# Second MLP product of an encoder layer: seven block products in place of eight, weight blocks summed by accumulating transfers

## The chip, the core and the metric

The kernel runs on one core of one Trainium2 chip. The metric is the device time of one execution in microseconds (us), taken as the median of several runs. The core has a matmul engine (PE, with its weight loads shown apart as PEld), a vector engine (DVE), an engine for activations and copies (ACT), a general engine (POOL) and a queue processor (SP) that here only starts transfers. Each engine works through its own instructions strictly in the order in which they were written; between engines they wait for each other by semaphores.

## The reference, cut to what matters

The program is one layer of an encoder on 512 tokens of width 1024. The change concerns its last stage, a squared-ReLU MLP of 4096 hidden features:

```python
h = rmsnorm(x, g_pre_mlp[l]) * (1.0 + sc2) + sh2                  # 512 x 1024
f = jnp.square(jax.nn.relu(h @ w_mlp1[l])) @ w_mlp2[l]            # 1024 -> 4096 -> 1024
x = x + gt2 * rmsnorm(f, g_post_mlp[l])
```

All of it is float32. A product in full precision is made of three matmuls: each operand is split into a high part of fewer bits and the low rest, and high by high, high by low and low by high are summed.

## The kernel before, in words

The kernel is recorded as a list of operations with their buffers. A planner (`Plan.order`) then walks through a model of the five engines: at each step it takes, of the operations whose inputs are ready and whose buffer slots are free, the one that can start first, and among those that can start at about the same time the one with the longest path behind it. What comes out is a fixed order for each engine. Its costs are lines of a small function (`_cost`); for a transfer it counts the issue, 0.65 us, the bytes at 360 GB/s, and 1.05 us until it has landed. An operation recorded on `vp` is one for DVE that the planner may give to POOL where it ends sooner there. All matmuls that write one PSUM bank share one priority.

A weight tile of 128 x 512 is loaded by SP (`wload`), split into `whi` by a copy on ACT and into `wlo` by a subtraction on DVE (`lo_of`), and used by PE. `mm3` writes the three matmuls of one product. Buffers have tags with a number of slots each (`NB`): split weights take slots of `w` (9) and `wx` (12), temporaries of `cv` (22).

The MLP works in two halves of 2048 features. In each half, four chunks of 512 features are computed (banks `pm`; 96 matmuls of 512 columns a chunk, in the first chunk 192 of 256): ReLU on ACT into `r`, square on `vp`, and the split into `gh` on ACT and `gl` on `vp`. Then `w_2` is multiplied in two column halves (banks `pf`): for each of 16 tiles of 128 features the split hidden values of four token tiles are the stationary operands and the split weight tile is the moving one, so a pair `whi`, `wlo` feeds 4 x 3 matmuls. In all that is 2 x 2 x 16 x 4 x 3 = 768 matmuls of 512 columns. The first half is copied from PSUM to `fA` by ACT, the second is added to it by DVE. At the end, for each token tile, the sum of squares is taken by ACT, the gain `G2` is multiplied in by DVE, a root and a reciprocal follow, and two DVE instructions scale the two column halves and add the residual `xr`; SP stores each half.

Of the kernel before, what the change touches and what calls it, by code (L numbers as in the profile page):

```python
# [220 lines left out]


class Op:
    __slots__ = ("eng", "call", "dur", "lat", "preds", "succs", "bufs", "new", "n", "rt", "start", "prio", "idx", "move", "urgent", "table", "port", "alt")


class Plan:
# [4 lines left out]
    def __init__(self, nc):  # L232
        self.nc, self.ops, self.tags, self.cnt = nc, [], {}, 0
        self.bias = self.local = 0.0
        self.pools = {}


# [15 lines left out]
    def record(self, eng, call, writes, reads, dur, lat=0.0, after=()):  # L253
        op = Op()
        op.eng, op.call, op.idx = eng, call, len(self.ops)
        op.dur, op.lat, op.move, op.urgent, op.table = dur, lat, None, self.local, None
        op.port, op.alt = eng == "gp", None
        preds = set(after)
        for v in reads:
            for q, box in v.b.writes:  # L260
                if _meet(box, v.box):
                    preds.add(q)
        for v in writes:
            for lst in (v.b.writes, v.b.reads):
                for q, box in lst:
                    if _meet(box, v.box):
                        preds.add(q)
        for v in writes:

            v.b.writes = [(q, box) for q, box in v.b.writes if not _within(box, v.box)]  # L270
            v.b.reads = [(q, box) for q, box in v.b.reads if not _within(box, v.box)]
            v.b.writes.append((op, v.box))
        for v in reads:
            v.b.reads.append((op, v.box))
        preds.discard(op)
        op.preds, op.succs = list(preds), []
        op.bufs = list({id(v.b): v.b for v in list(writes) + list(reads)}.values())
        op.new = []
        for b in op.bufs:
            if b.left == 0:  # L280
                op.new.append(b)
                self.tags[b.pool, b.tag]["order"].append(b)
            b.left += 1
            self.pools[b.pool]["left"] += 1
        op.prio = self.bias
        self.ops.append(op)
        return op


    def order(self):  # L290
# [14 lines left out]
        top = {}  # L305
        for op in ops:
            if op.eng == "pe":
                b = id(op.bufs[0])
# [246 lines left out]
def tile_hymba_layer(ctx, tc, t, out):  # L555
    nc = tc.nc
    plan = Plan(nc)

    FILTERS, INPUT, SOON, ROUND = 200.0, 1000.0, 9000.0, 3000.0
# [803 lines left out]


    w_1, w_2 = t["w_mlp1"][0], t["w_mlp2"][0]
    htag = (["cv"] * 3 + ["vx"]) * 6 + ["cv", "cv", "vx", "vx", "vx", "vx", "H", "vx"]
    hn = [0]

    def hidden_tile(s):
        hn[0] += 1  # L1370
        return R(htag[hn[0] % 32], s)

    fA, sq = {}, {}
    G2 = [S("G", "G2"), S("G", "G2")]
    late2 = ada_bcast(5120, t["g_post_mlp"][0], G2, ("ra",))
    step(late2)
    for half in range(2):
        hid = []
        for cc in range(4):
            c0 = half * 2048 + cc * 512  # L1380
            banks = PS4(cc + 1, "pm")
            ws = [wload(w_1[k * P:(k + 1) * P, c0:c0 + 512]) for k in range(8)]
            for th in range(2) if half == 0 and cc == 0 else (None,):
                ts = slice(0, 512) if th is None else slice(th * 256, th * 256 + 256)
                for k in range(8):
                    for i in range(4):
                        s = slice(i * P, (i + 1) * P)
                        mm3(banks[i][:, ts], ws[k][0][:, s], ws[k][1][:, s], h2T[k][0][:, ts], h2T[k][1][:, ts], k == 0, k == 7)
            for i in range(4):
                r = S("cv", "r")  # L1390
                act.activation(r, banks[i], AF.Relu)
                vp.tensor_tensor(out=r, in0=r, in1=r, op=ALU.mult)
                hi, lo = hidden_tile("gh"), hidden_tile("gl")
                act.copy(hi, r)
                lo_of(vp, lo, r, hi)
                hid.append((hi, lo))
            step(late2)
        for hf in range(2):
            cs = slice(hf * 512, hf * 512 + 512)
            banks = PS4(hf + 1, "pf")  # L1400
            nk = 8 if (half, hf) == (1, 1) else 16
            for k in range(nk):
                r0 = half * 2048 + k * P
                wh, wl = wload(w_2[r0:r0 + P, cs])
                for tt in range(4):
                    s = slice(tt * P, (tt + 1) * P)
                    mm3(banks[tt], hid[k][0][:, s], hid[k][1][:, s], wh, wl, k == 0, k == 15)
            if nk < 16:
                ws = [wload(w_2[half * 2048 + k * P:half * 2048 + (k + 1) * P, cs]) for k in range(nk, 16)]
            for tt in range(4):  # L1410
                s = slice(tt * P, (tt + 1) * P)
                for k in range(nk, 16):
                    mm3(banks[tt], hid[k][0][:, s], hid[k][1][:, s], ws[k - nk][0], ws[k - nk][1], False, k == 15)
                a = fA.get((tt, hf))
                if half == 0:
                    a = fA[tt, hf] = S("H", "fA")
                    act.copy(a, banks[tt])
                    continue
                dve.tensor_tensor(out=a, in0=banks[tt], in1=a, op=ALU.add)
                if hf == 0:  # L1420

                    q = sq[tt] = T1("sf")
                    act.activation(junk, a, AF.Square, accum_out=q[:, 0:1])
                    dve.tensor_scalar(out=q[:, 1:2], in0=q[:, 0:1], scalar1=1.0 / D, scalar2=EPS, op0=ALU.mult, op1=ALU.add)
                    vp.tensor_tensor(out=a, in0=a, in1=G2[0], op=ALU.mult)
                    continue
                q, g = sq[tt], S("cv", "g")
                act.activation(junk, a, AF.Square, accum_out=q[:, 2:3])
                dve.tensor_tensor(out=g, in0=a, in1=G2[1], op=ALU.mult)
                act.activation(q[:, 3:4], q[:, 2:3], AF.Sqrt, bias=q[:, 1:2], scale=1.0 / D)  # L1430
                dve.reciprocal(q[:, 4:5], q[:, 3:4])
                for i, a in enumerate((fA[tt, 0], g)):
                    dve.scalar_tensor_tensor(out=a, in0=a, scalar=q[:, 4:5], in1=xr[tt, i], op0=ALU.mult, op1=ALU.add)
                    sp.dma_start(out2d[tt * P:(tt + 1) * P, i * 512:(i + 1) * 512], a)

    done = plan.order()
    with tc.manual_schedule():
# [39 lines left out]
```

## Time and profile before

| | us |
|---|---|
| median of 3 runs (751.42 to 752.01) | 751.7 |
| the profiled execution | 750.51 |
| its span, first to last instruction | 748.7 |

The profile lists busy time by engine, groups of instructions by operation and tile, the chain of waits that ended last, and windows of the span. A name such as `pf<-whi,gh` reads: written tile, then what was read. All operations are issued from one helper line (L513), so tiles, not lines, tell the groups apart. The MLP begins at 375 us (first `pm` matmul) and is almost alone on PE from 396 us to the end.

### The profile page before, as it was taken

Reading aid. Unit: us, or ns where it says so; the run is one execution under the profiler, and the core shown is the slowest. Engines: PE = TensorE matmul, PEld = TensorE weight load, DVE = VectorE, ACT = ScalarE, POOL = GpSimd, SP = SyncE. Lnnn points to the kernel's source line nnn. Section 1 sums busy time; section 2 is a strip of 40 time slices with the busy share of each in tenths; the row PEclk is TensorE's granted clock in tenths of the full one; section 3 lists DMA queues with packets and bytes.
Section 4 is the critical chain, followed back from the end, with each engine's and each line's share of the span. In section 5 each row is a group of like instructions: output and inputs, shape, how many; then the busy total and the mean of one; then the engine's idle time right before and its main releaser. Section 6 shows DMA issues by size and latency. Waiting matters only on the chain.

```text
span 748.7 us, 10200 instructions
## 1 busy us (share of the span) xinstructions
PE 722.3 (96%) x3648; PEld 583.7 (78%) x3648; DVE 463.9 (62%) x884; ACT 325.1 (43%) x631; POOL 83.7 (11%) x82
## 2 busy tenths in 40 slices
PE   4999999999999999999989999999999999999995
PEld 1657878988888867778888888888888878888884
DVE  5498974989698778998878643323223363332256
ACT  4545452234224368988666333222323363222132
POOL 0120400113031133331120000000000000000000
PEclk9999999999999999999999999999999999999998
DMA  9996335433625363443124622223223343123212
GB/s 282 357 394 202 88 124 186 108 117 100 205 70 153 107 204 108 127 145 96 55 72 129 208 74 97 85 71 90 80 85 98 99 155 98 43 82 112 98 48 112
DMA packets 55603, 96.68 MB, mean 129 GB/s; under 512 B 5854, under 2 KB 14302, under 8 KB 55297
## 3 DMA queue, kind: packets, MB, share of 16 engines
q1 hardware_dynamic: 54400, 91.58, 38.7%
q0 software_dynamic: 1008, 4.40, 1.6%
q8 instruction: 28, 0.46, 0.2%
q14 instruction: 23, 0.18, 0.1%
q10 hardware_dynamic: 144, 0.06, 0.0%
HBM read 91.56 MB, written 4.46 MB: 128 GB/s over the span
## 4 chain that ended last, share of the span: by engine, by line
PE 83%; DVE 9%; DMA 4%; ACT 2%; issue 1%; SPq 0%; POOL 0%; DVEq 0%; ACTq 0%
PE pm L513 24%; PE pf L513 22%; PE pj L513 16%; PE pw L513 4%; PE pH L513 3%; PE pav L513 2%; PE inv L513 2%; PE ptr L461 2%; PE s L473 2%; PE pe L513 2%; DMA raw<-in_w_ada_dram 2%; PE po L513 1%; DMA raw<-in_w_out_dram 1%; DVE y L513 1%; DMA x<-in_x_dram 1%
## 5 line engine op out<-in xcount | busy, mean ns | idle before, releaser
L513 DVE TENSOR_TENSOR wlo<-raw,whi 128x512 fp32r<-128x512 f32 x176 | 120.0, 693 | 164.5 <-ACT whi L513 93.7
L513 ACT CAST whi<-raw 128x512 fp32r<-128x512 f32 x192 | 117.0, 620 | 189.9 <-PE pf L513 92.3
L513 PE MATMUL pm<-h2h,whi 128*128 128x512 f32 (+1 forms) x288 | 90.9, 373 | 2.2 <-DVE y L513 2.1
L513 PE MATMUL pm<-h2l,whi 128*128 128x512 f32 (+1 forms) x288 | 90.7, 372 | 0.3 <-POOL h2l L513 0.3
L513 PE MATMUL pm<-h2h,wlo 128*128 128x512 f32 (+1 forms) x288 | 90.4, 373 | 0.0
L513 PE MATMUL pf<-whi,gl 128*128 128x512 f32 x256 | 85.4, 389 | 0.0
L513 PE MATMUL pf<-wlo,gh 128*128 128x512 f32 x256 | 84.8, 390 | 0.1
L513 PE MATMUL pf<-whi,gh 128*128 128x512 f32 x256 | 84.2, 391 | 0.0
L513 PEld LDWEIGHTS pm<-h2h,whi 128*128 128x128 f32 x288 | 53.4, 191 | 12.9 <-DVE y L513 2.3
L513 PEld LDWEIGHTS pm<-h2l,whi 128*128 128x128 f32 x288 | 53.5, 191 | 10.5 <-POOL h2l L513 0.5
L513 PEld LDWEIGHTS pm<-h2h,wlo 128*128 128x128 f32 x288 | 53.0, 190 | 10.3 <-DVE wlo L513 0.5
L513 PEld LDWEIGHTS pf<-whi,gh 128*128 128x128 f32 x256 | 47.8, 188 | 11.3 <-ACT r L513 0.6
L513 PEld LDWEIGHTS pf<-wlo,gh 128*128 128x128 f32 x256 | 47.5, 188 | 11.1 <-DVE wlo L513 0.5
L513 PEld LDWEIGHTS pf<-whi,gl 128*128 128x128 f32 x256 | 48.1, 188 | 10.2
L513 DVE SCALAR_TENSOR_TENSOR acc<-raw,vec,acc 128x512 f32<-128x512 f32 x56 | 44.6, 796 | 10.2 <-DMA raw<-in_w_ada_dram 9.9
L513 DVE TENSOR_TENSOR r<-r 128x512 f32<-128x512 f32 x32 | 21.6, 688 | 40.5 <-ACT r L513 40.5
L513 ACT ACTIVATE r<-pm 128x512 f32<-128x512 f32 x32 | 18.4, 596 | 54.0 <-PE pm L513 54.0
L513 PE MATMUL pj<-hl,whi 128*128 128x512 f32 x96 | 36.1, 401 | 0.0
L513 PE MATMUL pj<-hh,whi 128*128 128x512 f32 x96 | 35.2, 397 | 0.7 <-ACT hh L513 0.7
L513 PE MATMUL pj<-whi,hh 128*128 128x512 f32 x96 | 35.1, 399 | 0.4 <-DVE y L513 0.4
L513 PE MATMUL pj<-hh,wlo 128*128 128x512 f32 x96 | 35.4, 397 | 0.0
L513 PE MATMUL pj<-wlo,hh 128*128 128x512 f32 x96 | 34.9, 399 | 0.0
(246 smaller groups left out, 1339.3 us busy)
## 6 DMA issues: line engine op xcount, KB each, us to landing
raw<-in_w_mlp_dram SPq DMA_DIRECT2D x128, 256.0 KB, 2.9
raw<-in_w_ada_dram SPq DMA_DIRECT2D x96, 256.0 KB, 3.4
raw<-in_w_in_dram SPq DMA_DIRECT2D x48, 256.0 KB, 3.2
raw<-in_w_out_dram SPq DMA_DIRECT2D x16, 256.0 KB, 2.9
H<-hd SPq DMA_DIRECT2D x9, 256.0 KB, 5.2
x<-in_x_dram SPq DMA_DIRECT2D x8, 256.0 KB, 5.1
hd<-H SPq DMA_DIRECT2D x8, 256.0 KB, 2.5
xr<-in_x_dram SPq DMA_DIRECT2D x8, 256.0 KB, 4.2
```

The source lines that it names most:

```text
L461: plan.nc.tensor.transpose(out.ap()[:, i * P:(i + 1) * P], v.ap(), ident.ap())
L473: plan.nc.tensor.matmul(out.ap(), ts[i][0].ap(), ts[i][1].ap(), start=i == 0, stop=i == n - 1)
L513: getattr(e, meth)(*[real(a) for a in args], **{k: real(a) for k, a in kw.items()})
```

## The change: what it does

The hidden features are taken in four groups of 1024 in place of two of 2048. The second product of one group is a product of a 512 x 1024 matrix A (tokens by features) with a 1024 x 1024 matrix B. Both are cut into 2 x 2 blocks: A11 and A12 are the first 256 tokens, A21 and A22 the others; the first index of B counts feature blocks of 512, the second the output columns in halves. In place of the eight block products there are seven, numbered as in the code and computed in this order:

- 4: (A21 - A22) by B00
- 2: A22 by (B00 + B10)
- 1: (A11 - A21 + A22) by (B00 + B10 + B11)
- 3: A11 by B01
- 6: (A21 - A11) by (B00 + B10 + B11 + B01)
- 5: A12 by B11
- 7: (A12 - A11 + A21 - A22) by (B11 + B10)

Each has 4 tiles of features, 2 token tiles and 3 matmuls of 512 columns, so a pair `whi`, `wlo` feeds 6 matmuls. All four groups together make 4 x 7 x 24 = 672. The sums of B are formed in the loaded tile `braw`: B00 is loaded by SP, split, then B10 is added into the same tile by an accumulating transfer that POOL issues, the sum is split again, and so on (`load`, `more`). That makes 48 loads by SP and 64 accumulating transfers, and 112 splits of `w_2` tiles in place of 64. Differences of A (`dif`) are formed by `vp`, 16 of 256 columns a group, and each A operand of a product is split into one tile `ha` (high part left, low part right), 28 a group, in place of one split of 512 columns for each hidden tile.

The products of the first group are copied to 14 accumulators by ACT, those of the second and third are added there by DVE (28 additions). Before the last group the accumulators are combined (16 additions on `vp`), so that each product of the last group is added to the one or two outputs that it belongs to (24 additions by DVE). The ending of each token tile is the same as before, in another order. The priority of a `pf` bank now counts for one block product alone (`group`), and each chunk and group gets a lead of 30 in priority over the next (`LEAD`).

The order on PE becomes: chunks 1, 2, 3, group 1, chunks 4, 5, group 2, chunks 6, 7, group 3, chunk 8, group 4, with a few matmuls interleaved at each border.

```diff
             if op.eng == "pe":
-                op.prio = top[id(op.bufs[0])]
+                op.prio = top[id(op.bufs[0]), op.group]
...
-        for hf in range(2):
-            cs = slice(hf * 512, hf * 512 + 512)
-            banks = PS4(hf + 1, "pf")
-            nk = 8 if (half, hf) == (1, 1) else 16
-            for k in range(nk):
-                r0 = half * 2048 + k * P
-                wh, wl = wload(w_2[r0:r0 + P, cs])
-                for tt in range(4):
-                    s = slice(tt * P, (tt + 1) * P)
-                    mm3(banks[tt], hid[k][0][:, s], hid[k][1][:, s], wh, wl, k == 0, k == 15)
...
+    def put(n, i, bank):
+        if (n, i) in acc:
+            dve.tensor_tensor(out=acc[n, i], in0=bank, in1=acc[n, i], op=ALU.add)
+        else:
+            acc[n, i] = S(ATAG[len(acc)], "acc") if len(acc) < 12 else spare.pop()
+            act.copy(acc[n, i], bank)
...
+    def split_w(raw):
+        hi, lo = wpair()
+        act.copy(hi, raw)
+        lo_of(vp, lo, raw, hi)
+        return hi, lo
+    def split_a(src):
+        a = R("cv", "ha")
+        act.copy(a[:, 0:256], src)
+        lo_of(vp, a[:, 256:512], src, a[:, 0:256])
+        return a
...
+    TO = {1: ((7, 1), (6, 1)), 2: ((2, 1), (6, -1)), 3: ((6, 1), (5, 1)), 4: ((2, 1), (7, 1)), 5: ((7, -1), (5, 1)),
+          6: ((6, 1),), 7: ((7, 1),)}
...
+            for k in range(KT):
+                wh, wl = split_w(raws(k))
+                a = parts(k)
+                for i in range(2):
+                    mm3(banks[i], a[:, i * P:(i + 1) * P], a[:, 256 + i * P:256 + (i + 1) * P], wh, wl, k == 0, k == KT - 1)
+            for i in range(2):
+                arrive(n, i, banks[i])
...
+        def load(key, r, c):
+            def get(k):
+                B[key, k] = S("wx", "braw")
+                sp.dma_start(B[key, k], wsrc(r, k, c))
+                return B[key, k]
+            return get
+        def more(key, r, c):
+            def get(k):
+                pool.dma_start(B[key, k], wsrc(r, k, c), accum_op=ALU.add)
+                return B[key, k]
+            return get
...
+        product(4, diff(0, A21, A22), load("s", 0, 0))
+        product(2, same(A22), more("s", 1, 0))
+        product(1, diff(0, A11, D0), more("s", 1, 1))
+        product(3, same(A11), load("b", 0, 1))
+        product(6, diff(1, A21, A11), more("s", 0, 1))
+        product(5, same(A12), load("d", 1, 1))
+        product(7, diff(0, A12, D0), more("d", 1, 0))
```

Up to the first chunk of the MLP all five engines have the same instructions in the same order as before. Three places behind it show what moves.

On POOL, the last instructions of the program before, which belong to the start of the MLP:

```order
L513 TENSOR_TENSOR wlo_4286<-raw_4139,whi_4264 128x512
L513 TENSOR_TENSOR wlo_4323<-raw_4159,whi_4307 128x512
L513 TENSOR_TENSOR wlo_4337<-raw_4194,whi_4319 128x512
L513 TENSOR_TENSOR h2l_4191<-h_4407,h2h_4183 128x256
L513 TENSOR_TENSOR h2l_4252<-h_4441,h2h_4245 128x256
```

and the last ones now, in the fourth group (`G` is the gain `G2`, the four `braw` at the end are the tiles of product 7):

```order
L514 TENSOR_TENSOR dif_6837<-r_7159,dif_6837 128x256
L514 TENSOR_TENSOR acc_5047<-acc_5047,G_4460 128x512
L514 TENSOR_TENSOR ha_7324<-r_7149,ha_7324 128x256
L514 TENSOR_TENSOR acc_5210<-acc_5210,G_4460 128x512
L514 TENSOR_TENSOR ha_7360<-dif_6782,ha_7360 128x256
L514 TENSOR_TENSOR ha_7372<-dif_6786,ha_7372 128x256
L514 TENSOR_TENSOR ha_7365<-r_7159,ha_7365 128x256
L514 TENSOR_TENSOR ha_7383<-dif_6797,ha_7383 128x256
L514 DMA braw_7375<-in_w_mlp_dram 128x512
L514 DMA braw_7390<-in_w_mlp_dram 128x512
L514 DMA braw_7396<-in_w_mlp_dram 128x512
L514 DMA braw_7433<-in_w_mlp_dram 128x512
```

POOL had nothing in the MLP behind its first chunk; it now issues 64 transfers there and does some of DVE's work between them: 9 instructions of 256 columns and 2 of 512 stand between the last transfer but four and these four.

On DVE, the rows from the low part of product 5's first weight tile to that of product 7's first, in the fourth group; both are made from `braw_7375`, and between them lie the first subtraction, the accumulating transfer and the copy to `whi_7469` on ACT (`pf` are banks of products 3, 5 and 6):

```order
L514 TENSOR_TENSOR wlo_7425<-braw_7375,whi_7412 128x512
L514 TENSOR_TENSOR wlo_7435<-braw_7390,whi_7421 128x512
L514 TENSOR_TENSOR wlo_7441<-braw_7396,whi_7430 128x512
L514 TENSOR_TENSOR acc_5282<-acc_5282,pf_7367 128x512
L514 TENSOR_TENSOR acc_5300<-acc_5300,pf_7326 128x512
L514 TENSOR_TENSOR acc_5429<-acc_5429,pf_7326 128x512
L514 TENSOR_TENSOR ha_7408<-dif_6837,ha_7408 128x256
L514 TENSOR_TENSOR g_7465<-acc_5282,G_5009 128x512
L514 TENSOR_TENSOR wlo_7471<-braw_7433,whi_7460 128x512
L514 TENSOR_SCALAR sf_7282<-sf_7282 128x1
L514 TENSOR_SCALAR sf_7303<-sf_7303 128x1
L514 TENSOR_TENSOR wlo_7479<-braw_7375,whi_7469 128x512
```

Before, no weight tile was written twice: each `wlo` waited for one load that SP had started long ahead. Now the last row waits for a transfer that could start only after the first row.

On DVE, the end of the program before, from the addition of the last result of PE (`pf_6839`):

```order
L513 TENSOR_TENSOR fA_6074<-pf_6839,fA_6074 128x512
L513 TENSOR_TENSOR g_7050<-fA_6074,G_5379 128x512
L513 RECIPROCAL sf_6908<-sf_6908 128x1
L513 SCALAR_TENSOR_TENSOR fA_5570<-fA_5570,sf_6908,xr_3640 128x512
L513 SCALAR_TENSOR_TENSOR g_7050<-g_7050,sf_6908,xr_3648 128x512
```

and now, from the addition of the last result of PE (`pf_7536`; `rope` and `mask` are old buffers that serve as accumulators):

```order
L514 TENSOR_TENSOR rope_590<-rope_590,pf_7536 128x512
L514 RECIPROCAL sf_7523<-sf_7523 128x1
L514 TENSOR_TENSOR g_7568<-rope_590,G_4460 128x512
L514 SCALAR_TENSOR_TENSOR acc_5210<-acc_5210,sf_7303,xr_3640 128x512
L514 SCALAR_TENSOR_TENSOR g_7499<-g_7499,sf_7303,xr_3648 128x512
L514 RECIPROCAL sf_7545<-sf_7545 128x1
L514 SCALAR_TENSOR_TENSOR acc_5404<-acc_5404,sf_7523,xr_3588 128x512
L514 SCALAR_TENSOR_TENSOR g_7557<-g_7557,sf_7523,xr_3581 128x512
L514 SCALAR_TENSOR_TENSOR acc_5429<-acc_5429,sf_7545,xr_3602 128x512
L514 SCALAR_TENSOR_TENSOR g_7568<-g_7568,sf_7545,xr_3595 128x512
```

Behind the last matmul there stood two instructions that scale and add the residual; there are six now.

More of the change, by code (lines that the diff above doesn't have):

```diff
@@ L223 @@
 class Op:
-    __slots__ = ("eng", "call", "dur", "lat", "preds", "succs", "bufs", "new", "n", "rt", "start", "prio", "idx", "move", "urgent", "table", "port", "alt")
+    __slots__ = ("eng", "call", "dur", "lat", "preds", "succs", "bufs", "new", "n", "rt", "start", "prio", "idx", "move", "urgent", "table", "port", "alt", "group")
 class Plan:
@@ L234, in __init__ @@
         self.bias = self.local = 0.0
+        self.group = 0
         self.pools = {}
@@ L256, in record @@
         op.dur, op.lat, op.move, op.urgent, op.table = dur, lat, None, self.local, None
-        op.port, op.alt = eng == "gp", None
+        op.port, op.alt, op.group = eng == "gp", None, self.group
         preds = set(after)
@@ L307, in order @@
             if op.eng == "pe":
-                b = id(op.bufs[0])
+                b = id(op.bufs[0]), op.group
                 top[b] = max(top.get(b, 0.0), op.prio)
@@ new lines, in tile_hymba_layer, with hidden @@
+    acc, ATAG = {}, ["H"] * 9 + ["G"] + ["cv"] * 2
+    spare = [rope.rearrange("p a b c -> p (a b c)"), mask[:, 0:512]]
+    def put(n, i, bank):
[4 more added lines that the diff above has]
+            act.copy(acc[n, i], bank)
+    def hidden(cc, banks):
+        ws = [wload(w_1[k * P:(k + 1) * P, cc * 512:cc * 512 + 512]) for k in range(8)]
+        for th in range(2) if cc == 0 else (None,):
+            ts = slice(0, 512) if th is None else slice(th * 256, th * 256 + 256)
+            for k in range(8):
+                for i in range(4):
+                    s = slice(i * P, (i + 1) * P)
+                    mm3(banks[i][:, ts], ws[k][0][:, s], ws[k][1][:, s], h2T[k][0][:, ts], h2T[k][1][:, ts], k == 0, k == 7)
+        res = []
+        for i in range(4):
+            r = S("vx", "r")
+            act.activation(r, banks[i], AF.Relu)
+            vp.tensor_tensor(out=r, in0=r, in1=r, op=ALU.mult)
+            res.append(r)
+        return res
@@ new lines, in split_w, with early_half @@
+    def split_w(raw):
[8 more added lines that the diff above has]
+        return a
+    def early_half(tt, a, hf):
+        q = T1("sf")
+        act.activation(junk, a, AF.Square, accum_out=q[:, 0:1])
+        dve.tensor_scalar(out=q[:, 1:2], in0=q[:, 0:1], scalar1=1.0 / D, scalar2=EPS, op0=ALU.mult, op1=ALU.add)
+        vp.tensor_tensor(out=a, in0=a, in1=G2[hf], op=ALU.mult)
+        return q
@@ new lines, in late_half @@
+    def late_half(tt, a, hf, q, other):
+        g = S("cv", "g")
+        act.activation(junk, a, AF.Square, accum_out=q[:, 2:3])
+        dve.tensor_tensor(out=g, in0=a, in1=G2[hf], op=ALU.mult)
+        act.activation(q[:, 3:4], q[:, 2:3], AF.Sqrt, bias=q[:, 1:2], scale=1.0 / D)
+        dve.reciprocal(q[:, 4:5], q[:, 3:4])
+        for i, o in ((1 - hf, other), (hf, g)):
+            dve.scalar_tensor_tensor(out=o, in0=o, scalar=q[:, 4:5], in1=xr[tt, i], op0=ALU.mult, op1=ALU.add)
+            sp.dma_start(out2d[tt * P:(tt + 1) * P, i * 512:(i + 1) * 512], o)
@@ new lines, in tile_hymba_layer, with begin, next_hidden @@
+    TO = {1: ((7, 1), (6, 1)), 2: ((2, 1), (6, -1)), 3: ((6, 1), (5, 1)), 4: ((2, 1), (7, 1)), 5: ((7, -1), (5, 1)),
+          6: ((6, 1),), 7: ((7, 1),)}
+    NS, KT = 4, 4
+    HALF = (slice(0, 256), slice(256, 512))
+    NCC = 2 * NS
+    hid, piece = {}, [0]
+    def begin():
+        plan.local = LEAD * (NCC + NS - piece[0])
+        piece[0] += 1
+        return piece[0] % 2
+    def next_hidden():
+        cc = len(hid)
+        if cc < NCC:
+            hid[cc] = hidden(cc, PS4(begin(), "pm"))
+            step(late2)
```

116 lines of the change are left out of this document (63 added, 53 removed).

## The prediction

> **What bounds the kernel now.** I read the busy time by engine first, then windows of the MLP, then the groups of instructions there, then the last lines of the chain of waits and the timeline.
>
> ```profile
> span 748.7 us, 10200 instructions
> PE 722.3 (96%) x3648; PEld 583.7 (78%) x3648; DVE 463.9 (62%) x884; ACT 325.1 (43%) x631; POOL 83.7 (11%) x82
> 460.00:500.00 40.00, 40.00 (x177) 32.86 (x176) 9.82 (x15) 8.39 (x14) 0.00 (x0) 1.00 0.27 86
> 500.00:540.00 40.00, 40.00 (x175) 32.34 (x174) 13.15 (x20) 12.64 (x22) 0.00 (x0) 1.00 0.26 80
> 580.00:620.00 40.00, 40.00 (x173) 32.22 (x172) 21.36 (x34) 18.30 (x33) 0.00 (x0) 1.00 0.39 126
> 660.00:700.00 40.00, 39.92 (x175) 32.33 (x174) 9.64 (x15) 8.70 (x14) 0.00 (x0) 1.00 0.31 98
> 711.64 22.48 PE pf L513 x98
> ```
>
> The window rows give start and end, length, then busy time and count for PE, PEld, DVE, ACT and POOL, the granted clock (1.00 is full), the DMA share and GB/s. The reader is to see that PE has no gap in the MLP, at full clock, while DVE is busy a quarter to a half of the time and POOL not at all. Four windows of 40 us hold 177 + 175 + 173 + 175 = 700 matmuls, so one takes 160 / 700 = 0.2286 us from start to start; the piece of the chain above gives 22.48 / 98 = 0.2294. I take 0.229. The kernel before is bound by the number of matmuls, and nothing else is near.
>
> **The change, part by part.**
>
> *Matmuls.* 768 become 672 of the same form (the 512 weight columns move, 128 token columns stand). 96 x 0.229 = **-22.0 us**, if PE stays without gaps. The weight loads that lie beside them stay 32 of 40 us in those windows. The rest of the sum is what takes PE's density away.
>
> *What the other engines do for it.*
>
> ```profile
> L513 DVE TENSOR_TENSOR wlo<-raw,whi 128x512 fp32r<-128x512 f32 x176 | 120.0, 693 | 164.5 <-ACT whi L513 93.7 <-PE pf L513 44.4 <-PE pm L513 19.9
> L513 ACT CAST whi<-raw 128x512 fp32r<-128x512 f32 x192 | 117.0, 620 | 189.9 <-PE pf L513 92.3 <-PE pm L513 51.1 <-PE pj L513 27.9
> L513 DVE TENSOR_TENSOR h2l<-h,h2h 128x256 fp32r<-128x256 f32 x14 | 5.7, 445 | 1.4 <-ACT h2h L513 1.3
> L513 ACT CAST h2h<-h 128x256 fp32r<-128x256 f32 x16 | 5.8, 404 | 0.9 <-DVE h L513 0.6
> L513 ACT ACTIVATE r<-pm 128x512 f32<-128x512 f32 x32 | 18.4, 596 | 54.0 <-PE pm L513 54.0
> 719.40 2.49 DVE L513 TENSOR_TENSOR fA<-fA,G 128x512 f32<-128x512 f32 x4
> ```
>
> Four DVE instructions of 512 columns in a row take 2.49 us, so each takes 0.62 when DVE is full, though its own time is 0.69. For 256 columns, 0.445 less the same 0.07 gives 0.38 (estimate). DVE's order now falls into stretches between the ReLU squares of successive chunks. Between chunk 3 and 4 (group 1 and a chunk: 264 matmuls, 60.5 us on PE) stand 42 instructions of 512 columns and 32 of 256: 38 us. Between chunk 5 and 6: 55 x 0.62 + 30 x 0.38 = 45.5 of 60.5. Between chunk 7 and 8: 69 x 0.62 + 29 x 0.38 = 54 of 60.5, and POOL adds five. ACT has 44, 36 and 34 us there. On average PE stays the bound in the first three groups, but the margin in the third is a few us, and orders are fixed, so one late instruction holds all behind it. Bounds 0 and the size of that margin, 6; I take **+2**, nearer 0, since before every such row waited for PE (the releasers in the rows above), not the other way.
>
> *The fourth group* has no chunk to hide behind. After the last `pm` matmul PE has 165 left, 37.8 us. DVE starts with two squares and a difference (ReLU 0.6, then 0.62 + 0.38 + 0.69: 2.4 us) and then has 51 instructions of 512 columns, 14 of 256, 8 that scale and add, and 8 tiny ones.
>
> ```profile
> 740.29 0.39 PE L513 MATMUL pf<-whi,gl 128*128 128x512 f32 x1
> 741.92 0.69 DVE L513 TENSOR_TENSOR fA<-pf,fA 128x512 f32<-128x512 f32 x1
> 743.73 0.17 DVE L513 RECIPROCAL sf<-sf 128x1 f32<-128x1 f32 x1 [0.39 <-ACT sf L513]
> 743.92 0.75 DVE L513 SCALAR_TENSOR_TENSOR fA<-fA,sf,xr 128x512 f32<-128x512 f32 x1
> 744.59 0.75 DVE L513 SCALAR_TENSOR_TENSOR g<-g,sf,xr 128x512 f32<-128x512 f32 x1
> ```
>
> Two scale-and-adds start 0.67 apart. 31.6 + 5.3 + 5.4 + 0.7 = 43 us, so DVE ends at 2.4 + 43 = 45.4 us without one wait. PE's own path ends at 37.8 plus what follows its last result. Before, that was 740.68 to 745.34, 4.7 us. Now an addition, a product, two reciprocals and six scale-and-adds follow: 2 x 0.62 + 0.3 + 6 x 0.67 + 0.2 = 5.8. So the ending is **+1.1** longer, PE's path is 43.6, and DVE's is 1.8 beyond it. POOL takes 9 + 2 instructions there that would have been DVE's; whether that helps is seen here:
>
> ```profile
> 384.92 3.05 POOL L513 TENSOR_TENSOR wlo<-raw,whi 128x512 fp32r<-128x512 f32 x2 [3.46 <-ACT whi L513]
> 385.27 3.25 DVE L513 SCALAR_TENSOR_TENSOR xr<-y,ry,xr 128x512 f32<-128x512 f32 x2
> 395.60 0.73 POOL L513 TENSOR_TENSOR h2l<-h,h2h 128x256 fp32r<-128x256 f32 x1 [7.62 <-ACT h2h L513]
> ```
>
> Two DVE instructions that need 1.4 us took 3.25 while POOL worked: each waited for POOL's. POOL's eleven take 9 x 0.73 + 2 x 1.5 = 9.6 us. Against DVE's 24 additions from PSUM (15 us) they may be free. Bounds: 0 (DVE's waits elsewhere cover its surplus) and 1.8 + 9.6 = 11.4. I take 1.8 and about a sixth of POOL's time, **+3.5**.
>
> The Trainium skill, page "SBUF — State Buffer", section "Who interferes with whom", says that a DVE instruction with two SBUF inputs and a GpSimd instruction that reads SBUF exclude each other for a whole instruction. The 3.25 us agree. By that rule alone, all 9.6 us would add where DVE's neighbours read SBUF; that case is a rival below.
>
> *Accumulating transfers.* The trace has none. The nearest rows:
>
> ```profile
> raw<-in_w_mlp_dram SPq DMA_DIRECT2D x128, 256.0 KB, 2.9
> fb<-in_c_fb_dram POOLq DMA_DIRECT2D x1, 1536.0 KB, 9.1
> nb<-in_c_nb_dram POOLq DMA_DIRECT2D x4, 256.0 KB, 9.4
> 35.02 0.73 POOL L513 DMA_DIRECT2D fb<-in_c_fb_dram  x1
> 35.74 1.60 POOL L513 DMA_DIRECT2D nb<-in_c_nb_dram  x3
> ```
>
> Let D be the time from issue to landing. An SP load of the same bytes took 2.9 us; a POOL load of them 9.4 us, but queued behind six times as much (`fb`, 1536 KB in 9.1 us). 9.1 / 6 = 1.5 us for 256 KB; if the addition reads the old tile as a second stream of that cost, D = 2.9 + 1.5 = 4.4. I take 4.5, nearer 2.9 because the `nb` row holds mostly queueing, and keep 2.9 and 9.4 as bounds. Behind each transfer follow ACT's copy (0.62), DVE's subtraction (0.69) and handovers of about 0.1, so a tile is ready D + 1.6 after the last read of the old sum. What covers this is PE's work from the first use of a tile to that of its next sum. In the fourth group 24 matmuls, 5.5 us, lie between the first use of `whi_7412` (product 5) and of `whi_7469` (product 7); from product 4 to 1 there are about 32 (7.3 us), from 1 to 6 about 43 (9.9 us). The excess per group is what D + 1.6 has over 5.5, 7.3 and 9.9: at D = 4.5 it is 0.6, 0 and 0, four groups give **+2.4**. At 2.9 it is 0; at 9.4 it is 5.5 + 3.7 + 1.1 = 10.3, or 41 us in all. While ACT waits at such a copy, its later splits stand behind it, and DVE's behind those.
>
> The Trainium skill, page "Collectives: The Full Stack", section "The bandwidth ceiling: the fold count and why AG ≠ RS ≠ AR", says that an addition in a transfer costs a second source read, and gives about 31 GB/s for an engine. By an estimate from that, the second read of 256 KB on 16 engines adds 0.5 us, D would be 3.4, this term 0 and the result 736.3. No run so far shows an addition in a transfer.
>
> **Sum**, against the profiled execution of 750.5: -22.0 + 2 + 3.5 + 1.1 + 2.4 = -13.0, so 737.5. The median of the runs shown is 1.2 above the profiled one, so 751.7 - 13.0 = **738.7 us**.
>
> **The rivals.**
>
> *Everything hides.* PE shows no gap in the windows before, and the new work is on average below PE's in three groups. Then only DVE's 1.8 and the ending's 1.1 are left, or the ending alone: 751.7 - 22.0 + 1.1 = 730.8, up to 732.6. Against it: the fourth group's arithmetic leaves DVE no room. Chance 0.15.
>
> *POOL and DVE exclude each other throughout.* 11.4 instead of 3.5, and 4 more in the first three groups: 738.7 + 11.9 = 750.6 at most, about 747 if a third of it meets additions from PSUM. Chance 0.12, mostly still faster.
>
> *Slower: the accumulating transfer's latency sets the pace.* The same sum with the chain term open is -15.4 + 4 x excess. It reaches 0 at 3.85 a group, (D - 3.9) + (D - 5.7), so at D = 6.7 us. At D = 8 it is 751.7 - 15.4 + 25.6 = 762; at 9.4 it is 777.5. For it: the only POOL loads of this size took 9.4, and eleven POOL instructions stand ahead of the last four transfers. Against it: those loads queued, and here the queue holds a few tiles at a time. Chance 0.15.
>
> *It doesn't do what it says:* the matmuls no longer stream at 0.229 us since operands change every six. But each matmul had its own weight load before too, 0.19 us under 0.229. 0.03.
>
> **How the numbers follow.** The forecast, 733 to 745, has 0.55: terms of 0 to 6, 0 to 11.4 and 0 to about 6 (D to 5.3) seldom all go one way. The range runs from 731 (nearly all of "everything hides") to 752 (most of the exclusion case), and leaves out the slower case and a little below. Against a measurement that can tell 0.2% (1.5 us) from no change: faster 0.82, same 0.03, slower 0.15.
>
> **What would show it.** PE's count of matmuls is 96 lower. In windows of the groups PE's count per 40 us stays at 170 or more in the first three and falls in the fourth, where DVE is above 90% busy. The table of transfers gives D for `braw` on POOL: under 5 is the forecast, over 6.7 the slower case, with ACT `whi` waiting for DMA and PE waiting for `whi` in the list of waits. POOL beside DVE shows as `wlo` means above 0.75 us. Wrong would be a gap in PE at the borders of groups that no transfer and no full DVE explains, or a later start of the MLP.

## The result, and the profile after

The changed kernel takes 758.3 us (median of 6 runs, 755.6 to 760.9) where the kernel before takes 751.6 on the same chip: a ratio of 1.0095, with a 95% interval of 1.0068 to 1.0122. It is slower by about 1%; the forecast was 738.7 us, and 752 the end of its range. The profiled execution took 759.21 us, with a span of 757.3.

The page, the windows of the MLP, and the table of transfers of the changed kernel (columns as before: start and end, length, PE, PEld, DVE, ACT, POOL, granted clock, DMA share, GB/s):

```profile
span 757.3 us, 10569 instructions
PE 708.6 (94%) x3552; PEld 564.6 (75%) x3552; DVE 573.2 (76%) x1113; ACT 375.7 (50%) x765; POOL 162.6 (21%) x169
460.00:500.00 40.00, 37.52 (x160) 29.25 (x159) 24.70 (x46) 27.85 (x57) 7.25 (x9) 1.00 0.66 158
500.00:540.00 40.00, 40.00 (x174) 32.15 (x173) 20.86 (x43) 14.51 (x31) 2.84 (x4) 1.00 0.36 105
580.00:620.00 40.00, 40.00 (x174) 32.29 (x173) 25.82 (x51) 17.38 (x36) 3.12 (x3) 1.00 0.39 125
700.00:740.00 40.00, 32.59 (x132) 25.08 (x131) 36.00 (x54) 19.00 (x43) 18.50 (x20) 0.96 0.59 123
q0 software_dynamic: 10224, 21.18, 15.2%
braw<-in_w_mlp_dram POOLq DMA_DIRECT2D x64, 256.0 KB, 4.6
braw<-in_w_mlp_dram SPq DMA_DIRECT2D x48, 256.0 KB, 3.0
```

PE has its 96 matmuls less (3552 for 3648). Where chunks run (500 to 540, 580 to 620), PE is as dense as before, 174 per 40 us. Where a group's products run, it isn't: 160 in 460 to 500, and 132 in the fourth group's window. The median accumulating transfer lands 4.6 us after its issue: the forecast had taken 4.5. The waits in the MLP, in total, times and longest:

```profile
ACT whi L514 <- DMA braw<-in_w_mlp_dram: 66.2, 50, 5.7
PEld pf L514 <- ACT whi L514: 16.2, 15, 2.4
PE pf L514 <- ACT whi L514: 10.5, 9, 2.0
PEld pf L514 <- DVE acc L514: 6.9, 5, 4.6
PE pf L514 <- DVE acc L514: 5.9, 4, 4.2
```

Before, the weight loads of the second product waited for `whi` twice, 0.4 us in all. Now ACT stands 50 times at a copy whose tile hasn't landed, and PE behind it. The timeline of the first group shows how, rows of POOL and SP (issues), ACT and PE (start, duration, in brackets the idle time ahead and what ended it):

```profile
451.06 2.74 POOL L514 DMA_DIRECT2D braw<-in_w_mlp_dram  x3 [0.57 <-DVE wlo L514]
455.54 0.62 ACT L514 CAST whi<-braw 128x512 fp32r<-128x512 f32 x1 [1.74 <-DMA braw<-in_w_mlp_dram]
457.76 0.62 ACT L514 CAST whi<-braw 128x512 fp32r<-128x512 f32 x1 [1.60 <-DMA braw<-in_w_mlp_dram]
458.43 0.96 PE L514 MATMUL pf<-whi,ha 128*128 128x512 f32 x3 [1.64 <-ACT whi L514]
...
462.28 2.69 POOL L514 DMA_DIRECT2D braw<-in_w_mlp_dram  x3 [2.02 <-DVE wlo L514]
463.55 5.54 SPq L514 DMA_DIRECT2D braw<-in_w_mlp_dram  x4
466.14 0.86 POOL L514 DMA_DIRECT2D braw<-in_w_mlp_dram  x1 [1.16 <-ACT ha L514]
470.31 0.62 ACT L514 CAST whi<-braw 128x512 fp32r<-128x512 f32 x1 [2.32 <-DMA braw<-in_w_mlp_dram]
470.98 0.98 PE L514 MATMUL pf<-whi,ha 128*128 128x512 f32 x3 [2.02 <-ACT whi L514]
```

The reader is to see two stalls of PE, each right behind a copy that waited for a transfer. At the first, three accumulating transfers of product 2 and 1 had been issued together; by the trace's landings they came at 455.5, 457.7 and 459.0, 2.2 and 1.3 us apart, so the last took 6.0 us. At the second the copy waits for an ordinary load by SP, product 3's: it went out at 463.55 among four accumulating transfers of product 6, which landed at 466.0, 471.0, 473.0 and 475.0, the slowest after 9.2 us. One of SP's loads in that burst took 8.2 us.

From PE's rows I add up what is missing: consecutive matmuls in the MLP start 0.229 us apart, and where they start more than 0.29 apart, the time over 0.229 is missing (a matmul whose record is lost counts 0.23). By quarters of the `pf` matmuls, which are the four groups (nearly so where the fourth has 192), with the time from the last matmul's start to the span's end:

| profiled execution of | group 1 | 2 | 3 | 4 | ending |
|---|---|---|---|---|---|
| the kernel before, whole stage | 1.5 in all | | | | 8.4 |
| the changed kernel | 5.7 | 5.7 | 5.2 | 11.2 | 11.1 |
| e3, no sums | 0.1 | 1.2 | 0.6 | 2.4 | 10.2 |
| e4, transfers that don't add | 0.0 | 2.4 | 1.3 | 8.0 | 11.1 |
| e5, transfers priced | 2.3 | 3.7 | 6.4 | 7.2 | 9.5 |
| e18, priced, don't add | 0.1 | 0.2 | 1.9 | 6.7 | 9.7 |
| e13, priced and spaced | 0.4 | 2.7 | 3.0 | 12.2 | 9.4 |
| e14, priced, without POOL | 2.0 | 0.7 | 2.6 | 8.7 | 8.7 |
| e10, sums by engines, last plain | 0.0 | 1.6 | 5.6 | 0.0 | 8.6 |

In the changed kernel 27.8 us are missing and the ending is 2.6 longer, where the matmuls brought 96 x 0.229 = 22.0. With the 1.5 missing before, that is 27.8 - 1.5 + 2.6 - 22.0 = 6.9 of the 8.6 us by which the span grew.

### The profile page after: what moved, and what is told of

The parts are those of the page before. It is cut to its first block, busy times and chain, and to the rows that moved or that the text cites. A ratio compares the mean times of both kernels' runs of the same rounds, so it can differ in the third digit from the quotient of the medians.

```text
span 757.3 us, 10569 instructions
## 1 busy us (share of the span) xinstructions
PE 708.6 (94%) x3552; PEld 564.6 (75%) x3552; DVE 573.2 (76%) x1113; ACT 375.7 (50%) x765; POOL 162.6 (21%) x169
## 3 DMA queue, kind: packets, MB, share of 16 engines
q0 software_dynamic: 10224, 21.18, 15.2%
## 5 line engine op out<-in xcount | busy, mean ns | idle before, releaser
L514 PE MATMUL pf<-whi,ha 128*128 128x512 f32 x448 | 135.2, 398 | 18.5 <-ACT whi L514 10.5
L514 DVE TENSOR_TENSOR wlo<-braw,whi 128x512 fp32r<-128x512 f32 x112 | 78.8, 725 | 55.4 <-ACT whi L514 49.3
L514 PEld LDWEIGHTS pf<-whi,ha 128*128 128x128 f32 x448 | 83.5, 190 | 44.1 <-ACT whi L514 16.2
L514 ACT CAST whi<-braw 128x512 fp32r<-128x512 f32 x112 | 67.6, 619 | 82.8 <-DMA braw<-in_w_mlp_dram 66.6
L514 ACT CAST whi<-raw 128x512 fp32r<-128x512 f32 x128 | 77.1, 619 | 58.3 <-PE pj L514 27.9
L514 POOL DMA_DIRECT2D braw<-in_w_mlp_dram x64 | 55.9, 929 | 212.5 <-DVE wlo L514 116.4
L514 DVE TENSOR_TENSOR wlo<-raw,whi 128x512 fp32r<-128x512 f32 x111 | 75.9, 698 | 22.4 <-ACT whi L514 10.7
L514 PE MATMUL pf<-wlo,ha 128*128 128x512 f32 x224 | 79.0, 396 | 1.6 <-DVE wlo L514 1.6
L514 PEld LDWEIGHTS pf<-wlo,ha 128*128 128x128 f32 x224 | 42.2, 189 | 13.5 <-DVE wlo L514 4.9
L514 POOL TENSOR_TENSOR sc<-sc,st 128x512 f32<-128x512 f32 x21 | 24.0, 1160 | 55.5 <-DVE st L514 47.6
```

The source lines that it names most:

```text
L514: getattr(e, meth)(*[real(a) for a in args], **{k: real(a) for k, a in kw.items()})
```

## The experiments

Each kernel is the changed one with the edit shown. The kernel before, run beside them, stood at 749.8 to 750.3 us, where it stood at 751.6 beside the changed kernel. Differences between medians of separate sets of runs, as below, are therefore known to 1 or 2 us at best.

**The two suspects alone: POOL beside DVE, and the sums (e1 to e4).** e1 takes POOL's arithmetic away.

```diff
+        vp = dve
         A11, A21 = [[a[:, h] for a in aa] for h in HALF]
```

> The products' splits, differences and additions are recorded for DVE alone, so POOL only issues transfers in the groups. Changed kernel: 758.3 us; its PE loses about 14.3 us in gaps in groups 1 to 3 and 10.5 us in group 4. Theory 'shared port' (POOL's arithmetic holds DVE, as where one 0.42-us instruction took 4.63): the long gap of 4.3 us in group 4 and about half of the others there go, 5 to 8 us: 750 to 753 us, groups 1 to 3 as they were. Theory 'latency of the accumulating transfers': within 2 us of 758, since DVE gets 5 to 6 us more work in group 4.

Measured: 760.3 us (759.8 to 766.2). No gain; the missing time of the four groups is 6.3, 5.4, 4.9 and 10.1 us. Giving POOL's arithmetic to DVE doesn't make this kernel faster, though in group 4 it looks as if it should:

```profile
710.40 4.63 DVE L514 TENSOR_TENSOR ha<-r,ha 128x256 fp32r<-128x256 f32 x1
710.40 1.07 POOL L514 TENSOR_TENSOR ha<-dif,ha 128x256 fp32r<-128x256 f32 x1
711.10 1.06 POOL L514 TENSOR_TENSOR ha<-r,ha 128x256 fp32r<-128x256 f32 x1
711.79 1.73 POOL L514 TENSOR_TENSOR dif<-r,dif 128x256 f32<-128x256 f32 x2
713.17 1.56 POOL L514 TENSOR_TENSOR acc<-acc,G 128x512 f32<-128x512 f32 x1
716.87 1.22 PE L514 MATMUL pf<-whi,ha 128*128 128x512 f32 x2 [4.18 <-DVE acc L514]
```

These rows of the changed kernel show a DVE instruction of 0.42 us that stands for 4.63 while five of POOL's run back to back, and PE waiting 4.18 behind it. With POOL's arithmetic gone, PE still waits 5.5 us for DVE's additions in group 4 of e1: DVE has POOL's work to do instead.

e2 puts one other product between two uses of a sum, and handles 6 as the last product in place of 7.

```diff
-        4, 2 ("s"), 1 ("s"), 3, 6 ("s"), 5, 7 ("d")
+        4, 3, 2 ("s"), 5, 1 ("s"), 7 ("d"), 6 ("s")
```

> Products in the order 4,3,2,5,1,7,6 in place of 4,2,1,3,6,5,7: between two uses of the same sum stands one other product, so 11 us of PE's work cover each accumulating transfer where 5.5 us did. Theory 'latency': PE's gaps of groups 1 to 3 (14.3 us, waits for whi) shrink to 0 to 4 us: 744 to 749 us. Theory 'shared port': the gaps stay or move, 755 to 760 us.

Measured: 772.0 us (768.0 to 773.1), 14 more than the changed kernel, against both theories. In its profile PE waits for ACT's copies of PSUM banks (`acc`) too, 5.5 us in all, which stand in ACT's queue among the splits. Left unexplained here; e13 takes it up.

e3 and e4 take the additions out in two ways.

```diff
# e3, for each of the four sums of a group
-        product(2, same(A22), more("s", 1, 0))
+        product(2, same(A22), load("s", 1, 0))
# e4
-                pool.dma_start(B[key, k], wsrc(r, k, c), accum_op=ALU.add)
+                pool.dma_start(B[key, k], wsrc(r, k, c))
```

> Leaves out the sums of weight blocks: each product loads one plain block by SP into a tile of its own. No accumulating transfer, no chain; splits, products and additions are as many as before. Theory 'latency': groups 1 to 3 lose under 2 us and group 4 loses less: 738 to 745 us. Theory 'shared port' or 'DVE is full': 750 us or more, since DVE, ACT and POOL have the same arithmetic.

> Leaves out the addition in the transfers only: POOL issues a plain load over the same tile, in the same order with the same waits as the changed kernel. If it is the addition (second read) that makes them slow: landing falls from 4.6 to about 3 us and the queued ones from 8 to 5, the gaps of groups 1 to 3 fall by half, 748 to 753 us. If it is POOL's issue and its queue, or the chain itself: landing stays at 4 us or more and the time within 3 us of 758.

Measured: e3 733.8 us (733.5 to 735.1), below what any theory gave; e4 740.1 (739.7 to 741.8), also below both of its theories. Neither forms the sums. e4 has the changed kernel's order on every engine and the same waits. So 758.3 - 740.1 = 18.2 us are the addition inside the transfers, and 740.1 - 733.8 = 6.3 more go with the chain of transfers over one tile and the order made for it. If each is taken from the kernel before that ran beside it, the 18.2 become 16.9, and the 24.5 of both together 23.2. The table of transfers of e4:

```profile
q0 software_dynamic: 6128, 21.18, 8.6%
braw<-in_w_mlp_dram POOLq DMA_DIRECT2D x64, 256.0 KB, 3.5
```

Without the addition the median landing falls from 4.6 to 3.5 us (4.64 to 3.46), the slowest from 9.2 to 5.5, SP's slowest `braw` load from 8.2 to 5.2, and POOL's own time for an issue from 0.87 to 0.54. The packets of this queue fall from 10224 to 6128; the bytes that the profile counts for it stay at 21.18 MB.

**Order, place and means of the sums (e5 to e8).** e5 changes no transfer, only what the planner believes of them; e6 adds on engines; e7 adds in DRAM, ahead of the group; e8 takes the fourth group out.

```diff
# e5, in _cost
+        if kw.get("accum_op") is not None:
+            return 0.87, v.free * v.shp[0] * 4 / 150e3
# e6, in more
-                pool.dma_start(B[key, k], wsrc(r, k, c), accum_op=ALU.add)
+                raw = S("raw", "raw")
+                sp.dma_start(raw, wsrc(r, k, c))
+                add(vp, B[key, k], B[key, k], raw)
# e7, for each k, with e5's price
+            pool.dma_start(d[0], wsrc(0, k, 0), after=(first,))
+            pool.dma_start(d[0], wsrc(1, k, 0), accum_op=ALU.add)
+            pool.dma_start(d[1], d[0])
+            pool.dma_start(d[1], wsrc(1, k, 1), accum_op=ALU.add)
...
+                sp.dma_start(B[key, k], sums[k][j])
# e8, last group: split each of 8 hidden tiles once, then
+                    for tt in range(4):
+                        mm3(banks[tt], act8[k][0][:, s], act8[k][1][:, s], wh, wl, k == 0, k == 7)
```

> Only the planner's price of an accumulating transfer changes: 0.87 us of POOL and 1.75 us of the transfers' time for 256 KB, in place of 1.04 and 0.73 (the trace of the changed kernel: 0.87 to issue, landings about 1.8 us apart where several were under way). Theory 'the order was made for a transfer that is too short': ACT's and DVE's queues stand less behind a late copy, the gaps of groups 1 to 3 (16.6 us with the small ones) fall to about half: 748 to 753 us. Theory 'the chain itself and the tiles for splits ahead are the bound': within 2 us of 758, since the transfers take as long and the tiles are as many.

> The sums of weight blocks are formed by additions on DVE or POOL (the planner chooses) from plain loads by SP; no accumulating transfer. 64 additions of 0.62 us on DVE or 1.3 to 1.6 us on POOL more. Theory 'only the transfers were slow': groups 1 to 3 near 1 us of gaps each, group 4 about 10 more us of work for DVE and POOL: 742 to 750 us. Theory 'DVE has no room left and POOL holds it': group 3 (54 of 60.5 us taken) and group 4 pay 10 us each, 755 us or more.

> The same sums, formed by copies and accumulating transfers in DRAM ahead of their group (first group from about 300 us on, the others from a chunk or more before), then loaded by SP as plain tiles; the price of e5. The additions by transfers stay, 64 of them, and 64 copies come on top, but nothing in SBUF waits for them. Without any sum the run gave 733.8 us. Theory 'it is the chain of landing, split, next transfer that costs': 734 to 740 us. Theory 'it is the traffic (twice the packets) that slows every load': loads by SP stay at 4 us or more beside the sums, and gaps as large as before come back: 750 us or more.

> The fourth group alone as plain products like the kernel before (192 matmuls in place of 168, no sums; its additions from PSUM 8 in place of 24); groups 1 to 3 as in the changed kernel. 24 x 0.229 = 5.5 us more on PE; group 4's gaps (11.2 us) and the longer ending (2.6 us) go. Theory 'the last group lacks cover': 758.3 + 5.5 - 13.8 = 750 us. Theory 'all groups lose alike to the transfers' (about 5 us each): 758.3 + 5.5 - 5 to 8 = 756 to 759 us.

Measured: e5 747.1 us (743.3 to 751.1; ratio to before 0.9964, 0.9941 to 0.9987), e6 746.8 (742.1 to 748.6), e7 804.3 (801.6 to 809.8), e8 752.0 (748.5 to 755.7).

In e5 the transfers are the same and as long as before (median 4.8 us, slowest 8.8), but the order was made for a greater length, and 11.2 us are back (9.6 by the kernel before beside each):

```profile
braw<-in_w_mlp_dram POOLq DMA_DIRECT2D x64, 256.0 KB, 4.8
```

e6 needs no such transfer and comes out level with it, with DVE 24 us busier than in the changed kernel. e7 fits the theory of the traffic:

```profile
dsum<-in_w_mlp_dram POOLq DMA_DIRECT2D x96, 256.0 KB, 9.4
PEld pf L514 <- ACT whi L514: 34.1, 17, 5.8
```

The transfers into DRAM land after 9.4 us, loads by SP take up to 17 us, the sums come too late for groups 1 and 2 (29 and 19 us missing), and the MLP itself begins 31 us later than in the changed kernel (first `pm` matmul at 405.9 for 374.8). Groups 3 and 4, whose sums lay ready, miss only 1.3 and 2.8. e8 gives back 6.3 us, between its two theories: nothing is missing in the plain fourth group, but groups 2 and 3 still miss 6.6 and 6.1.

**The order once more, and combinations (e9 to e12).** e9 was meant to be e5 with e4's edit. But the price of e5 hangs on the addition and went with it, so e9's order is e4's and the run measures e4 a second time; e18, below, mends that. e10 is e6 with e8, e11 is e5 with e8, and e12 is e6 with e7's sums for group 4 alone.

> Order of e5 (the planner knows that the transfers are long); POOL's transfers write over the tile and add nothing (the sums are left out). With the changed kernel's order the addition cost 758.3 - 740.1 = 18.2 us. Theory 'the order decides how much of a slow transfer is paid': without the addition 736 to 742 us, so the addition costs only 5 to 10 us in this order. Theory 'the order of e5 is better in general, whatever the transfers do': 728 to 732 us, the addition costs 15 us or more here too.

> e6 (sums by additions on DVE or POOL, no accumulating transfer) with the fourth group as plain products of e8. From the profiles: last matmul of e6 at 735.8, less its group 4's gaps of 9.2, plus 24 matmuls (5.5 us), plus an ending of 9.1: 741 us. If the fourth group's plain products are slow beside engine sums of group 3 still under way: 745 us or more.

> e5 (price) with the fourth group as plain products of e8; accumulating transfers in groups 1 to 3 only. From the profiles: last matmul of e5 at 739.3, less 7.2 of gaps, plus 5.5, plus an ending of 9.1: 747 us, which is e5's own 747. If it comes out at 742 or less, the transfers of group 4 held group 3 too (6.4 us of gaps in e5).

> e6 in groups 1 to 3; the sums of group 4 alone are formed in DRAM between 450 and 640 us (16 copies, 16 accumulating transfers more than e6's none) and loaded as plain tiles. From the profiles: last matmul of e6 at 735.8, less 9.2 of gaps, plus 2.8 (group 4 of e7, whose sums were ready), plus an ending of 10.8: 740 us. If the traffic of the additions delays other loads as in the first groups of e7, or POOL's queue holds its arithmetic: 746 us or more.

Measured: e9 741.7 us (739.5 to 742.8), e10 739.0 (737.6 to 740.6), e11 750.9 (748.7 to 753.5), e12 750.9 (749.6 to 757.2). e10 is the fastest version with all of the sums in it: 0.9843 of before (0.9826 to 0.9860). Its page and two windows:

```profile
PE 708.2 (96%) x3576; PEld 569.4 (77%) x3576; DVE 570.6 (77%) x1106; ACT 364.8 (49%) x733; POOL 102.9 (14%) x96
460.00:500.00 40.00, 40.00 (x176) 32.65 (x175) 27.45 (x52) 24.53 (x50) 0.00 (x0) 1.00 0.55 173
700.00:730.00 30.00, 30.00 (x134) 24.85 (x133) 12.55 (x24) 5.80 (x15) 0.00 (x0) 1.00 0.15 53
```

PE is dense again in group 1 (176 per 40 us, for 160) and in group 4 (134 in 30 us). e11 is 3.8 us slower than e5, and e12 lost 4 against e6: its groups 1 to 3 miss 17.5 us where e6's miss 8.5, though only group 4's sums changed. Whether the traffic or the order did it was not separated.

**The square of order and addition (e18).** e18 has e5's order on every engine, and transfers that add nothing.

```diff
# against e5
-        if kw.get("accum_op") is not None:
+        if eng == "gp" and v.b.tag == "wx":
-                pool.dma_start(B[key, k], wsrc(r, k, c), accum_op=ALU.add)
+                pool.dma_start(B[key, k], wsrc(r, k, c))
```

> What e9 was meant to be: e5's order on every engine, with POOL's transfers writing over the tile and adding nothing (the sums are left out). In e9 the price hung on the addition and went with it, so e9 had e4's order and is a second measurement of e4 (741.7 and 740.1 us). Theory 'the order decides how much of a slow transfer is paid': without the addition 737 to 743 us, so the addition costs 4 to 10 us in this order where it cost 18.2 in the changed kernel's. Theory 'the order of e5 is better in general, whatever the transfers do': 728 to 733 us, the addition costs 14 us or more here too.

Measured: 737.3 us (735.8 to 739.1).

| | transfers add | they don't | the addition costs |
|---|---|---|---|
| order of the changed kernel | 758.3 | 740.1 (e4; 741.7 in e9) | 18.2 |
| order with the price of e5 | 747.1 | 737.3 (e18) | 9.8 |

Of the 11.2 us between the orders, 2.8 (by e9, 4.4) are there without any addition, so the new order is a little better in itself. The other 7 to 8 are the addition. Taken from the kernel before that ran beside each, the additions cost 16.9 and 10.0 us, the orders lie 9.6 apart, and the addition's part is 5 to 7. Either way the same slow transfers cost little more than half as much.

**Cover, and POOL again, with the price right (e13 to e17).** e13 is e2 with e5's price, e14 is e1 with it, e15 is e10 with e1's edit, e16 is e13 with e1's edit, e17 is e13 with e8.

> e2 (products in the order 4,3,2,5,1,7,6) with e5's price of the transfers. e2 alone gave 772, e5 alone 747. Theory 'the spaced order failed only because the planner priced the transfers too low': 740 to 747 us, since each sum has two products of cover. Theory 'the spaced order holds four tiles of s, of b and of d at once, 12 of the 21 that splits live in, so too few splits go ahead': 755 us or more, with the price right too.

> e5's price with the products' splits, differences and additions on DVE alone (e1's edit). If POOL's arithmetic beside DVE still costs in e5 (group 4: 7.2 us of gaps, 4.3 of them waits for DVE): 742 to 745 us. If it takes as much from DVE as it gives: 745 to 749 us, as e5. If DVE needs the help: 750 us or more.

> e10 (sums by engines, fourth group plain) with splits, differences and sums on DVE alone in the groups. e10: 739.0 us, with 5.6 us of gaps in group 3, where five of POOL's arithmetic instructions stood. If POOL holds DVE there: 733 to 736 us. If DVE is full in group 3 without POOL: 739 to 744 us.

> The spaced order with the price (e13) and the products' arithmetic on DVE alone (e14's edit). In e13 groups 1 to 3 lost 6.2 us of gaps and group 4 12.2 us, nearly all waits for DVE. If POOL's arithmetic holds DVE in group 4 as between e5 and e14 (4.2 us): 742 to 745 us. If the spaced order bunches DVE's additions at the end whatever POOL does: 746 to 750 us.

> e13 with the fourth group as plain products: accumulating transfers stay in groups 1 to 3, spaced and priced. Last matmul of e13 at 737.1, less 12.2 of gaps, plus 5.5, plus an ending of 8.6 to 9.1: 739 to 740 us, level with e10, which has no accumulating transfer. If so, transfers that add cost nothing once they are spaced and priced. If 745 us or more, spacing only moved the wait into the last group (as e11 stood to e5).

Measured: e13 748.4 us (746.9 to 750.5), e14 742.9 (742.0 to 745.8), e15 739.7 (738.8 to 741.9), e16 745.5 (744.2 to 746.0), e17 741.3 (740.0 to 744.2).

e13 is 24 us under e2, whose only other difference is the price, so e2 was slow for the order that the low price made, and not for a lack of tiles alone. e13 itself ends just above the range of its first theory. Its waits:

```profile
PEld pf L514 <- ACT whi L514: 2.5, 4, 1.1
PE pf L514 <- ACT whi L514: 0.9, 2, 0.7
PE pf L514 <- DVE mask L514: 8.5, 1, 8.5
```

With spacing and price together PE hardly waits for `whi` any more (0.9 us for 10.5); the gain is lost to one wait of 8.5 us for DVE's addition to an accumulator (`mask`) in the last group. With that group plain (e17) 741.3 is left, near e10's 739.0: in groups 1 to 3 accumulating transfers can nearly be hidden. The fourth group, without a chunk to run beside, misses 6.7 to 8.0 us even where the transfers add nothing (e18, e4 in the table), for 2.4 without the chain (e3). e14 gains 4.2 on e5, while e15 gains nothing on e10, and e16 gains 2.9 on e13: by their expectations e14 says that POOL's arithmetic costs, e15 that DVE is full without it, and e16 lies between its two.

## Why the prediction was wrong, step by step

*Matmuls, -22.0; groups 1 to 3, +2; group 4, +3.5; ending, +1.1.* These four make -15.4, and e3, which has all of the change but the sums, measured 733.8 - 750.3 = -16.5. Its missing time is 1.8 us in groups 1 to 3 and 2.4 in group 4, its ending 1.8 longer than before. Against these, and with the 1.5 us missing before left out of account, the last three were each right within 1.1 us, and so was the sum. The matmuls stream as taken, and DVE, ACT and POOL have the room that the sum gave them.

*Accumulating transfers, +2.4.* This is the step that failed. With the sums the kernel takes 758.3 - 733.8 = 24.5 us more (23.2 by the kernel before beside each), ten times the term. The time D from issue to landing came out right, 4.6 for 4.5, but in part by luck: it was made of 2.9 for a load and 1.5 for the addition, and the runs show 3.5 for a plain transfer by POOL (e4) and 1.2 for the addition. What was wrong is what the prediction made of D: "the excess per group is what D + 1.6 has over 5.5, 7.3 and 9.9; at D = 4.5 it is 0.6, 0 and 0". Three things were missing in it.

First, it took every transfer to take the median. They come in bursts of three or four, land 1.3 to 5.0 us apart in the two bursts above, and hold SP's loads up as well: 9.2 us for the slowest, 8.2 for a load; the slowest tenth took 6.9 us or more. Where nothing is added (e4) the slowest takes 5.5, and groups 1 to 3 miss 3.7 us in place of 16.6.

Second, "from product 4 to 1 there are about 32" matmuls, but product 2 uses the same sum between them. ACT's order for one tile in group 1, with the place of each row:

```
402 L514 CAST whi1176_4822<-braw1175_4788 128x512
415 L514 CAST whi1195_4965<-braw1175_4788 128x512
424 L514 CAST whi1211_5051<-braw1175_4788 128x512
439 L514 CAST whi1247_5159<-braw1175_4788 128x512
```

The four copies are for products 4, 2, 1 and 6, with a transfer before each but the first. Two of them lie in those 32 matmuls: by the prediction's own rule 2 x (4.6 + 1.6) - 7.3 = 5.1 us a group, close to the 5.2 to 5.7 that groups 1 to 3 miss. That this count is the cause is not shown, and the nearness is no proof. In PE's order of groups 1 to 3, product 1's first use of a tile stands 31 to 46 matmuls behind product 4's, and product 7's only 1 to 20 behind product 5's, where the prediction took the fourth group's 24 for all four. By the same rule that last link would miss up to 6 us more a group, which isn't there. The rule leaves out that the chain can start ahead of PE: in group 1 the first accumulating transfer went out at 432.9 us, and PE's first matmul of the group came at 452.6. Nor do the runs bear the count out: spacing alone (e2) made the kernel slower, and price alone helped without any spacing.

Third, the order was fixed for transfers of 3.47 us, 1.04 + 0.65 + 0.73 + 1.05 in the planner's price, whether they add or not; a plain one takes that (3.46 in e4), one that adds takes more. Where a copy on ACT waits for a late transfer, all that stands behind it in ACT's queue waits too. The prediction named that in one sentence and gave it no price. A greater length in the planner's table gave 11.2 us back (e5), 5 to 8 of them by paying less for the additions, though the slowest transfer still took 8.8 us. In the spaced order the same edit gave 24 us (e2 to e13). But with the fourth group plain it gave about 1 (e8 to e11, 752.0 to 750.9). So it is shown that the order decides how much of a slow transfer is paid, and not that the right length always makes a better one.

*The two rules that the prediction weighed.* The Trainium skill, page "Collectives: The Full Stack", section "The bandwidth ceiling: the fold count and why AG ≠ RS ≠ AR", says of the reduce step of a collective that its addition costs a second source read. The packet counts here fit that: (10224 - 1008) / 64 = 144 for a transfer that adds, (6128 - 1008) / 64 = 80 for one that doesn't, 1008 being those of e3. The counted bytes don't show it, 21.18 MB in both. The prediction's estimate of 0.5 us from it was too low for the median, which rose by 1.2, and far too low for a burst. The Trainium skill, page "SBUF — State Buffer", section "Who interferes with whom", says that DVE instructions with two SBUF inputs and POOL's reads exclude each other; the means of one DVE form in the last group, from 690 us on, agree, 0.734 us in e5 and 0.417 in e14:

```profile
L514 DVE TENSOR_TENSOR ha<-dif,ha 128x256 fp32r<-128x256 f32 x10 | 6.9, 734 | 0.0
L514 DVE TENSOR_TENSOR ha<-dif,ha 128x256 fp32r<-128x256 f32 x10 | 4.1, 417 | 0.0
```

The first row is e5, with POOL's arithmetic beside it, the second e14, without. Still the 4.2 us between the two runs are not shown to be this: PE misses less in groups 2 and 3 and not less in group 4, the order of the splits changed with the edit, and e5's profiled execution was its longest, 4 us over its median.

*The rivals.* "The latency sets the pace" was the right one, at 0.15, and it put the turning point at D = 6.7 us. The kernel turned slower with a median of 4.6; neither bursts nor the queue behind a late copy were in that rule. "POOL and DVE exclude each other throughout" is not it: without POOL's arithmetic (e1) the kernel takes 760.3, and groups 1 to 3 miss as much as before (6.3, 5.4 and 4.9 us for 5.7, 5.7 and 5.2). What would show it, the prediction listed as D over 6.7 with ACT's `whi` waiting for transfers and PE for `whi`: the waits came, the D did not. PE's count, which it kept at 170 or more in the first three groups, fell to 160 already in the first.

*Open* is why e11 loses on e5 and why e12 loses on e6. Groups 1 to 3 of e11 miss 16.2 us, as many as those of e8 without the price, where e5's miss about 12. Each edit makes another order of the whole stage, and what the order alone did was not separated there. Open too is how the loss divides among the three points above.

## What to carry to other kernels

Price a new kind of instruction from a trace before a fixed order is made around it: the additions in the transfers cost 17 to 18 us in an order made for short ones and 10 in one made for their length. Measure the new order too, since it isn't better in every kernel (e8 to e11). For a chain through one tile, count every link between two uses, and take the slow tenth of the transfers in a burst (6.9 us here), not the median (4.6). In a stage without other work beside it, fewer dependences can be worth more work: plain products in the last group, with 24 more matmuls, gained 6 to 8 us in three kernels (e8, e10, e17) and lost 4 in one (e11).

## What the runs showed of the hardware

A transfer that adds into SBUF moves 144 packets in place of 80 for 256 KB, takes POOL 0.87 us to issue in place of 0.54, and the slowest of a burst of four landed after 9.2 us; ordinary loads issued among them took up to 8.2 us in place of 5.2.

After a stall, PE can run at half speed for some us. These are PE's rows of the changed kernel behind its longest gap, and the window around them:

```profile
717.89 0.63 PE L514 MATMUL pf<-wlo,ha 128*128 128x512 f32 x1
718.32 1.05 PE L514 MATMUL pf<-whi,ha 128*128 128x512 f32 x2
719.17 0.63 PE L514 MATMUL pf<-wlo,ha 128*128 128x512 f32 x1
716.00:720.00 4.00, 3.13 (x8) 2.49 (x9) 3.40 (x6) 2.37 (x7) 1.47 (x2) 0.57 0.23 43
```

The matmuls start 0.43 us apart in place of 0.23, at a granted clock of 0.57. A gap of 2.02 us (470.98, above) left the clock at 1.00; in e12 one of 1.96 us was followed by 0.57 over the next 4 us.
